# Low parts of the attention weights: an accumulating transfer in place of a subtraction on DVE

## The chip, the cores and the metric

The kernel runs on one core of one Trainium2 chip. The metric is the device time of one execution in microseconds (us), as a median over runs; less is better.

## The reference

Two blocks follow each other on 512 tokens of width 1024. The part that matters here is the first, a differential attention layer; the second is a feed-forward layer (ffn), a token mixer and another ffn, each added to x with a gate.

```python
def diff_attention_layer(x, norm_g, w_in, ..., w_out, layer_idx):
    h = rms_norm(x, norm_g)
    q, k, v, z = jnp.split(h @ w_in, 4, axis=-1)        # 1024 -> 4 x 2048
    q = rms_norm(q.reshape(b, s, 16, 2, 64), q_norm_g) * (64 ** -0.5)
    k = rms_norm(k.reshape(b, s, 16, 2, 64), k_norm_g)
    ...
    weights = probs[:, :, 0] - lam * probs[:, :, 1]     # two softmaxes a head
    ...
    o = o.reshape(b, s, BRANCH) * jax.nn.silu(z)
    return x + o @ w_out                                # 2048 -> 1024
```

Everything is float32.

## The kernel before

A product of two float32 matrices is made of three matmuls in the fp32r format: each operand is split into a high part, its rounding to fp32r, and a low part, what is left (`split`, line 105: ACT casts the high part, line 106; DVE subtracts it from the source, line 107). `mm3` (line 88) then adds high by high, high by low and low by high into one bank.

Weights come in tiles of 512 KB, 128 partitions by 1024 elements. `raw_w` (line 109) loads one on the queue of the engine SP into one of 3 buffers named raw; `split_w` (line 117) makes the tiles whi and wlo of it, of which there are 4 buffers each; `load_w` (line 114) does both. So a cast waits until PE has used the whi that lay in its buffer for the last time, and the next load of raw waits until the raw tile has been read.

Three shapes of products call `load_w`. `gemm_tok` (line 137) has tokens as output rows: with 4 weight tiles, it takes two of the four token tiles through all of the weights, then the other two, with 6 matmuls of 512 columns for each pair of a weight tile and a token tile. Where its argument `tail` is set, the last `tail` weight tiles are gone through one token tile after the other. `gemm_feat` (line 173) has features as output rows and uses each weight tile for 24 matmuls on end. `gemm_col` (line 187) is not used in attention.

The attention layer (line 633) starts with a hand-ordered first product (`start`, line 509, which splits its own weights at lines 560 and 567), and then makes four groups of four heads: `qk` for q and k (line 651), `vg` for v (line 718), `zg` for z (line 723), and `wo` for the output product (line 819). After a q or k product, ACT copies the result (line 671) and squares it, DVE sums, POOL raises the mean to the power -0.5 (line 305, tile rs) and scales the rows (line 678, tile qraw), both in POOL's one queue; PE transposes them later. v is copied by ACT (line 721), the output product is added to x by DVE (line 420). The scores, softmaxes and weighted sums of the group before (`attn`, line 735) are laid between the matmuls of these products.

The order of PE's work is set by the program: `tc.manual_schedule` holds for PE's engine alone, and `later` (line 67) with `spend` (line 71) puts the pieces of attention between the matmuls by a clock that counts matmuls (`self.now`) and the due times of `DL` (line 34). The other engines' order is made by the scheduler of the framework from the order in which the program issues and its own estimate of times. Each engine works through its queue in order. Transfers issued on POOL (`nc.gpsimd.dma_start`) stand in POOL's queue with its arithmetic; in attention these are the constants and the biases of the modulation (`bcast`, line 125).

Of the kernel before, what the change touches and what calls it, by code (L numbers as in the profile page):

```python
# [9 lines left out]
F32 = mybir.dt.float32  # L10
F32R = mybir.dt.float32r
AF = mybir.ActivationFunctionType
ALU = mybir.AluOpType
AX = mybir.AxisListType

P = 128
# [25 lines left out]
class Net:  # L42
# [4 lines left out]
    def __init__(self, ctx, tc, a):  # L47
        self.tc, self.nc, self.a = tc, tc.nc, a
        nc = self.nc
        pool = lambda name, bufs=1, **k: ctx.enter_context(tc.tile_pool(name=name, bufs=bufs, **k))  # L50
        self.const = pool("const")
        self.hp = pool("hp")
        self.wp = pool("wp", 4)
        self.wk = pool("wk", SLOTS)
        self.sp = pool("sp", 4)
        self.dram = pool("dram", 1, space=bass.MemoryType.DRAM)
        self.ps = pool("ps", 1, space=bass.MemoryType.PSUM)
        self.now, self.seq, self.tasks = 0.0, 0, []
        self.mod, self.ada_queue, self.ada_busy, self.scratch = {}, [], False, None

        self.ident = self.const.tile([P, P], F32, name="ident")
        self.mhalf = self.const.tile([P, 8], F32, name="mhalf")
        nc.vector.memset(self.mhalf, -0.5)
        self.x = [None] * NT
# [47 lines left out]
        return raw  # L112

    def load_w(self, src, kk, nn):
        return self.split_w(self.raw_w(src, kk, nn))

    def split_w(self, raw):
        _, kk, nn = raw.shape
# [748 lines left out]
    def ffn(self, s, win, wout, nxt):  # L867
        nc = self.nc
        sg, gT, gs = {}, {}, {}

        def gate(i):
            def done(bank, d0, d1):
                for o, d in ((d0[:, :256], bank), (d1, d1), (d0[:, 256:], d0[:, 256:])):
                    nc.scalar.activation(o, d, AF.Silu)
                sg[i] = d0, d1
            return done

        def up(i):
            def done(bank, *d):
                c = slice(0, 256), slice(256, 512)  # L880
                nc.vector.tensor_tensor(d[0][:, c[0]], bank, sg[i][0][:, c[0]], op=ALU.mult)
                nc.gpsimd.tensor_tensor(d[1], d[1], sg[i][1], op=ALU.mult)
                nc.gpsimd.tensor_tensor(d[0][:, c[1]], d[0][:, c[1]], sg[i][0][:, c[1]], op=ALU.mult)
                for n in range(2):
                    gT[2 * i + n] = d[n]
            return done

        if s == 2:
            self.ada(2, 2, 3.0)
        wts = [self.load_w(win[g * 512:(g + 1) * 512, c0:c0 + 256], 4, 256) for c0 in (0, FFN) for g in range(2)]  # L890
        sta = lambda n: lambda k: tuple(x[:, k % 4, n % 2 * P:n % 2 * P + P] for x in wts[n // 2 * 2 + k // 4])
        first = [self.tile("d0") for _ in range(2)]
        sg[0] = first

        def ev_up(n, bank):
            gT[n] = sg[0][n]
            nc.vector.tensor_tensor(gT[n], bank, gT[n], op=ALU.mult)

        self.gemm_quad([sta(n) for n in range(4)],
                       [lambda b, n=n: nc.scalar.activation(first[n], b, AF.Silu) for n in range(2)] +  # L900
                       [lambda b, n=n: ev_up(n, b) for n in range(2)])
        def split_g(k):
            if k not in gs:
                gs[k] = self.tile("gs", F32R), self.tile("gs", F32R)
                self.split(*gs[k], gT[k])

        def act(k, t):
            split_g(k)
            return tuple(g[:, t * P:(t + 1) * P] for g in gs[k])

        self.fast_feat([(win[:, c0 + i * 256:c0 + i * 256 + 256], fn(i))
                        for i in range(1, FFN // 256) for c0, fn in ((0, gate), (FFN, up))],
                       lambda: [split_g(k) for k in range(DL["gs"])])
        if s == 0:
            self.ada(1, 0, 2.5, True)
            self.ada(1, 1, 2.5, True)

        self.ada_wait((s, 2))
        self.norm_reset()
        for half in range(2):  # L920
            ev = self.gated_add(self.mod[s, 2], True, self.lazily(nxt) if half else None)
            self.gemm_tok(act, KF, wout[:, half * 512:half * 512 + 512], lambda t, b: ev(half, t, b), 4 if half else 0)
# [509 lines left out]
```

## Time and profile before

| | us |
|---|---|
| Median of 3 runs (1873.27 to 1878.37) | 1877.58 |
| The profiled execution | 1875.29 |
| Its span, first to last instruction | 1873.5 |
| PE busy | 1821.5 |
| DVE busy | 1405.7 |
| ACT busy | 929.3 |
| POOL busy | 393.4 |

Busy times overlap. PE is TensorE's matmuls, PEld its weight loads, DVE is VectorE, ACT ScalarE, POOL GpSimd; SP only issues transfers. A row of a group reads: line, engine, operation, out<-in by the program's names, the shapes, how often, busy time, mean ns of one, the idle time of the engine just before them, and after the arrow what ended it. In a timeline a row is the start, the length and the work, with the idle time before it in brackets. The granted clock is 1.00 for TensorE's upper level of 2.4 GHz and 0.50 for the lower of 1.2 GHz.

### The profile page before, as it was taken

The page shows a single profiled execution, that of the slowest core. Times are in us where ns is not written, and L with a number is a line of the kernel's source. Part 1 is how long each engine was busy: PE and PEld are TensorE (multiplying, and loading weights), DVE is VectorE, ACT ScalarE, POOL GpSimd, SP SyncE. Part 2 cuts the span into 40 slices and gives each one's busy share as a digit, 9 for nine tenths or more (in the row PEclk, how much of TensorE's full clock was granted, in tenths as well). Part 3 has the DMA queues.
Part 4 walks back from the last instruction along what each step waited for, and adds up shares of the span by engine and source line. Part 5 has one row for each costly group of instructions (what it writes and reads, how often), then busy time and mean ns, then how long its engine had stood idle before and what let it go on. Part 6 is the DMA issues. An engine that isn't in the chain of part 4 may idle for free.

```text
span 1873.5 us, 29082 instructions
## 1 busy us (share of the span) xinstructions
PE 1821.5 (97%) x10799; PEld 1604.6 (86%) x10799; DVE 1405.7 (75%) x2904; ACT 929.3 (50%) x1692; POOL 393.4 (21%) x376
## 2 busy tenths in 40 slices
PE   8999999999999999999999989999999999999997
PEld 5887878788888999998888778888888889999886
DVE  5568768776966899998365798787878789999633
ACT  5576575465653454553235745654433344554521
POOL 3213214042112122332030212212100112232000
PEclk9999999999999999999999999999999999999999
DMA  4534534625422233357324321222356333333331
GB/s 166 136 115 139 154 98 126 204 68 147 139 92 73 70 111 103 102 179 248 111 63 119 85 67 52 63 62 77 116 164 219 114 133 124 113 102 102 124 113 56
DMA packets 187618, 217.93 MB, mean 116 GB/s; under 512 B 9618, under 2 KB 129826, under 8 KB 187476
## 3 DMA queue, kind: packets, MB, share of 16 engines
q1 hardware_dynamic: 181892, 198.00, 34.8%
q0 software_dynamic: 5584, 18.08, 3.1%
q8 instruction: 85, 1.39, 0.3%
q14 instruction: 57, 0.47, 0.1%
HBM read 201.34 MB, written 2.11 MB: 109 GB/s over the span
## 4 chain that ended last, share of the span: by engine, by line
PE 81%; DVE 9%; issue 4%; ACT 2%; POOL 2%; DMA 2%; SPq 0%; POOLq 0%; DVEq 0%; ACTq 0%
PE acc L84 70%; PE sc L84 5%; DVE wlo L107 2%; PE av L84 2%; PE sc L95 2%; DVE cvy L1032 1%; PE tr L95 1%; PE tr L778 1%; POOL rs L305 1%; DMA raw<-in_l_w_in_dram 1%; PE tr L84 1%; DVE S L232 1%; DMA araw<-in_ada_w_dram 0%; ACT whi L106 0%; DVE hn L342 0%
## 5 line engine op out<-in xcount | busy, mean ns | idle before, releaser
L84 PE MATMUL acc<-hT,whi 128*128 128x256 f32 (+1 forms) x2704 | 642.2, 331 | 4.3 <-DVE d L266 2.8
L84 PEld LDWEIGHTS acc<-hT,whi 128*128 128x128 f32 x2704 | 447.4, 192 | 37.7 <-DVE d L266 3.2
L107 DVE TENSOR_TENSOR wlo<-raw,whi 128x1024 fp32r<-128x1024 f32 (+1 forms) x325 | 330.5, 1027 | 167.6 <-ACT whi L106 165.1
L84 PE MATMUL acc<-hT,wlo 128*128 128x256 f32 (+1 forms) x1352 | 440.8, 326 | 2.4 <-DVE wlo L107 2.3
L106 ACT CAST whi<-raw 128x1024 fp32r<-128x1024 f32 (+1 forms) x325 | 285.8, 880 | 314.1 <-PE acc L84 256.6
L84 PEld LDWEIGHTS acc<-hT,wlo 128*128 128x128 f32 x1352 | 258.4, 191 | 25.2 <-DVE wlo L107 3.4
L84 PE MATMUL acc<-whi,hT 128*128 128x512 f32 x768 | 268.1, 406 | 0.8 <-ACT hT L106 0.8
L305 POOL TENSOR_TENSOR rs<-ms,mhalf 128x8 f32<-128x8 f32 (+2 forms) x76 | 95.3, 1254 | 664.0 <-DVE ms L303 556.5
L84 PE MATMUL acc<-whi,gs 128*128 128x512 f32 x704 | 219.2, 390 | 1.8 <-DVE gs L107 1.8
L84 PE MATMUL acc<-T,whi 128*128 128x256 f32 x960 | 174.5, 283 | 0.0
L84 PEld LDWEIGHTS acc<-whi,hT 128*128 128x128 f32 x768 | 145.5, 190 | 31.4 <-DVE hT L107 1.9
L106 ACT CAST whi<-S 128x512 fp32r<-128x512 f32 x160 | 99.3, 621 | 117.5 <-DVE S L232 89.5
L84 PEld LDWEIGHTS acc<-whi,gs 128*128 128x128 f32 x704 | 132.0, 188 | 29.9 <-DVE gs L107 2.6
L84 PE MATMUL acc<-wlo,hT 128*128 128x512 f32 x384 | 151.6, 395 | 1.7 <-DVE wlo L567 1.7
L84 PEld LDWEIGHTS acc<-T,whi 128*128 128x128 f32 x960 | 149.7, 192 | 0.0
L107 DVE TENSOR_TENSOR wlo<-S,whi 128x512 fp32r<-128x512 f32 x160 | 140.4, 895 | 0.2 <-ACT whi L106 0.2
L84 PE MATMUL acc<-wlo,gs 128*128 128x512 f32 x352 | 137.0, 389 | 0.0
L84 PE MATMUL acc<-T,wlo 128*128 128x256 f32 x480 | 135.9, 283 | 0.0
L232 POOL TENSOR_TENSOR S<-raw,S 128x512 f32<-128x512 f32 x40 | 65.5, 1637 | 207.4 <-DVE S L232 188.1
L763 ACT ACTIVATE p<-p,mn 128x128 f32<-128x128 f32 (+3 forms) x128 | 71.1, 556 | 46.8 <-DVE mn L759 45.1
L84 PEld LDWEIGHTS acc<-T,wlo 128*128 128x128 f32 x480 | 92.1, 192 | 0.0
L467 DVE SCALAR_TENSOR_TENSOR aacc<-araw,silu_c,aacc 128x512 f32<-128x512 f32 x98 | 77.3, 788 | 13.8 <-DMA araw<-in_ada_w_dram 13.0
(294 smaller groups left out, 3086.1 us busy)
## 6 DMA issues: line engine op xcount, KB each, us to landing
raw<-in_ffn_w_in_dram SPq DMA_DIRECT2D x88, 512.0 KB, 3.6
raw<-in_l_w_in_dram SPq DMA_DIRECT2D x60, 512.0 KB, 4.0
araw<-in_ada_w_dram SPq DMA_DIRECT2D x112, 256.0 KB, 4.5
raw<-in_mix_w_in_dram SPq DMA_DIRECT2D x53, 512.0 KB, 3.9
raw<-in_ffn_w_out_dram SPq DMA_DIRECT2D x44, 512.0 KB, 3.7
raw<-in_l_w_out_dram SPq DMA_DIRECT2D x16, 512.0 KB, 3.7
ada<-in_ada_w_dram POOLq DMA_DIRECT2D x32, 256.0 KB, 4.0
ab<-in_ada_b_dram POOLq DMA_DIRECT2D x18, 256.0 KB, 3.9
```

Of the source, the lines that this page charges most:

```text
L84: self.nc.tensor.matmul(out, a, b, start=start, stop=stop, skip_group_check=onto)
L95: self.nc.tensor.transpose(out[:, j * P:(j + 1) * P], src(j), self.ident)
L106: return (self.nc.scalar.copy(hi, src), self.nc.vector.tensor_tensor(lo, src, hi.bitcast(F32), op=ALU.subtract))
L107: self.nc.vector.tensor_tensor(lo, src, hi.bitcast(F32), op=ALU.subtract))
L232: sub = lambda o, x, y, op=ALU.subtract, e=nc.vector: e.tensor_tensor(o, x, y, op=op)
L305: pin(nc.gpsimd.tensor_tensor(r[:, :n], ms[:, :n], self.mhalf[:, :n], op=ALU.pow))
L467: nc.vector.scalar_tensor_tensor(acc, raw, self.silu_c[:, k:k + 1], acc, op0=ALU.mult, op1=ALU.add)
L763: nc.scalar.activation(p_[m][:, :L], p_[m][:, :L], AF.Exp, bias=mn[:, m:m + 1], scale=-1.0, accum_out=st[:, m, b:b + 1])
L778: nc.tensor.transpose(tr[:, c * P:(c + 1) * P], p0[:, c * P:(c + 1) * P], self.ident)
L1032: nc.vector.scalar_tensor_tensor(y[:, j:], r[:, :S - j], cw[:, 3 - j, n:n + 1], y[:, j:], op0=ALU.mult, op1=ALU.add)
```

## The change

In attention, `load_w` no longer calls `split_w`. ACT casts the high part as before, and then writes the negated high part into the low part's tile. A transfer issued on POOL reads the weights from DRAM a second time and adds them to that tile. From the first ffn on (`ffn`, line 867) a flag sends `load_w` back to `split_w`; the weights of `start` and all that don't come through `load_w` stay as they were.

```diff
@@ __init__
         self.now, self.seq, self.tasks = 0.0, 0, []
+        self.by_dma = True
@@ load_w
     def load_w(self, src, kk, nn):
-        return self.split_w(self.raw_w(src, kk, nn))
+        raw = self.raw_w(src, kk, nn)
+        if not self.by_dma:
+            return self.split_w(raw)
+
+        hi = self.wp.tile([P, kk, nn], F32R, tag="whi", name="whi")
+        lo = self.wp.tile([P, kk, nn], F32R, tag="wlo", name="wlo")
+        self.nc.scalar.copy(hi, raw)
+        self.nc.scalar.mul(lo, hi.bitcast(F32), -1.0)
+        self.nc.gpsimd.dma_start(lo, src.rearrange("(k p) n -> p k n", p=P), accum_op=ALU.add)
+        return hi, lo
@@ ffn
+        self.by_dma = False
         if s == 2:
             self.ada(2, 2, 3.0)
```

## Rows read from the trace of the kernel before

**Rows 1.** The page: its span and PE's busy time.
```profile
span 1873.5 us, 29082 instructions
PE 1821.5 (97%) x10799; PEld 1604.6 (86%) x10799; DVE 1405.7 (75%) x2904; ACT 929.3 (50%) x1692; POOL 393.4 (21%) x376
```

**Rows 2.** A stretch: busy of PE, PEld, DVE, ACT, POOL; clock, DMA share, GB/s.
```profile
30.00:610.00 580.00, 565.66 (x2916) 475.72 (x2914) 410.83 (x869) 346.92 (x673) 146.41 (x114) 0.99 0.42 124
```

**Rows 3.** What PE waited for, 30 to 610 us: total, times, longest.
```profile
PE av L84 <- ACT wt L781: 5.3, 3, 2.1
PE tr L778 <- DVE qkl L695: 2.2, 1, 2.2
PE tr L778 <- DVE mn L759: 2.0, 1, 2.0
PE acc L84 <- DVE wlo L107: 1.4, 2, 1.1
PE sc L84 <- DVE qkl L695: 1.0, 1, 1.0
```

**Rows 4.** Groups of DVE and of ACT by shape, 30 to 610 us.
```profile
L107 DVE TENSOR_TENSOR wlo<-raw,whi 128x1024 fp32r<-128x1024 f32 x80 | 101.8, 1277 | 47.9 <-ACT whi L106 46.6 <-PE av L84 0.7
...
L106 ACT CAST whi<-raw 128x1024 fp32r<-128x1024 f32 x80 | 84.0, 1050 | 57.6 <-PE acc L84 52.9 <-DMA qkT<-qkT 1.7 <-DMA raw<-in_l_w_in_dram 1.5
```

**Rows 5.** Two stretches around 174 us, columns as in rows 2.
```profile
171.00:174.30 3.30, 1.28 (x11) 1.12 (x10) 3.27 (x9) 1.27 (x5) 2.19 (x2) 1.00 0.72 230
174.30:178.00 3.70, 3.70 (x11) 2.85 (x11) 2.67 (x10) 1.91 (x8) 0.00 (x0) 0.55 0.51 191
```

**Rows 6.** DMA queues and issues, 30 to 610 us; last number: us to landing.
```profile
q1 hardware_dynamic: 43016, 68.85, 40.5%
...
raw<-in_l_w_in_dram SPq DMA_DIRECT2D x57, 512.0 KB, 3.9
...
qkT<-qkl SPq DMA_DIRECT2D x32, 128.0 KB, 2.3
...
ab<-in_ada_b_dram POOLq DMA_DIRECT2D x6, 256.0 KB, 3.9
```

**Rows 7.** The chain that ended last, near 538 us.
```profile
538.21 14.98 PE acc L84 x66
```

**Rows 8.** Timeline of ACT, 36 to 60 us.
```profile
37.98 1.05 ACT L106 CAST whi<-raw 128x1024 fp32r<-128x1024 f32 x1 [1.00 <-PE acc L84]
...
51.58 0.59 ACT L671 COPY qraw<-acc 128x512 f32<-128x512 f32 x1 [5.68 <-PE acc L84]
```

**Rows 9.** Timeline of POOL, 30 to 60 us.
```profile
34.51 1.67 POOL L305 TENSOR_TENSOR rs<-ms,mhalf 128x8 f32<-128x8 f32 x1 [5.58 <-DVE ms L303]
...
39.98 2.62 POOL L305 TENSOR_TENSOR rs<-ms,mhalf 128x8 f32<-128x8 f32 x1
...
46.10 1.96 POOL L678 TENSOR_TENSOR qraw<-qraw,rs 128x512 f32<-128x512 f32 x1
```

**Rows 10.** Timeline of ACT, 56 to 90 us.
```profile
57.55 1.05 ACT L106 CAST whi<-raw 128x1024 fp32r<-128x1024 f32 x1
...
61.44 1.05 ACT L106 CAST whi<-raw 128x1024 fp32r<-128x1024 f32 x1
...
75.21 0.59 ACT L721 COPY v<-acc 128x512 f32<-128x512 f32 x1 [7.46 <-PE acc L84]
...
80.79 1.05 ACT L106 CAST whi<-raw 128x1024 fp32r<-128x1024 f32 x1
```

**Rows 11.** Timelines of ACT and of DVE, 564 to 582 us.
```profile
572.78 1.05 ACT L106 CAST whi<-raw 128x1024 fp32r<-128x1024 f32 x1
...
579.58 0.69 DVE L420 TENSOR_TENSOR x<-acc,x 128x512 f32<-128x512 f32 x1 [2.75 <-PE acc L84]
```

**Rows 12.** Instructions that read whi: ns of one, then first and last start.
```profile
L84 PEld LDWEIGHTS acc<-hT,whi x802: 186/192/193, 89.5 to 760.0; 128*128 128x128 f32 x161
```

**Rows 13.** Groups of POOL by shape, 30 to 610 us.
```profile
L125 POOL DMA_DIRECT2D ab<-in_ada_b_dram x6 | 3.7, 623 | 33.3 <-DVE co L767 21.6 <-PE sc L84 11.8
```

## The prediction, made before the changed kernel was run

> **What bounds the kernel now.** I read the page's busy times first: PE is busy for 1821.5 of 1873.5 us [rows 1]. Then a table by stage: in attention, taken here as 30 to 610 us of the span, PE is busy for 565.66 of 580 us, DVE for 410.83, ACT for 346.92, POOL for 146.41, and the DMA engines for 0.42 [rows 2]. So whatever DVE is relieved of, PE can give back 14 us at most here. Third, who PE waited for in that stretch [rows 3]: DVE in four lines (2.2, 2.0, 1.4 and 1.0 us, 6.6 together), ACT's copies of the transposed weights of attention in one (5.3 us). The low parts themselves (line 107) are the 1.4. The stage is bound by PE, and its order is fixed in the program, so that a late operand of PE is added to the time in full.
>
> **The change, part by part.** *Count.* load_w is called for 76 weight tiles before the first ffn switches the flag off: 28 for q and k without the first, 16 for v, 16 for z, 16 for the output product. The 80 casts and 80 subtractions in attention [rows 4] hold these and four of the ffn.
>
> *What goes.* 76 subtractions of 1.277 us [rows 4], 97 us of DVE. They lie beside PE's work. What PE gets back is between nothing and the 6.6 us of waits on DVE, plus a clock step: around 171 us PE stood for some 2 us behind DVE, and the next 3.7 us ran at a granted clock of 0.55, most of it at 1.2 GHz instead of 2.4 [rows 5], which costs 3.7 × 0.45 = 1.7 us. So 0 to 8.3 us; I take half, **-4**, since part of those DVE waits come from work that stays.
>
> *What ACT gets.* 76 negations of the same shape as the cast, 1.050 us each [rows 4]: 80 us on an engine with 233 us free in the stretch, beside PE's work. Each stands right behind its cast, so ACT's other work near a hand-over comes 1.05 us later. Next to be late are the copies that PE waits 5.3 us for [rows 3]. Bounds: none of it, or every one of the three waits longer by a cast and a negation (3 × 2.1 = 6.3); I take **+2.5**, as most copies stand far from a hand-over.
>
> *What POOL and the queues get.* 76 software-issued transfers of 512 KB on POOL's queue, which wait there for the negation. POOL's in-order work behind them is the normalization of q and k. No row shows an accumulating transfer. Nearest rows [rows 6]: 512 KB on SP's queue land in 3.9 us, 128 KB in 2.3, so 128 KB more cost 0.53 us, and 512 KB are 1.8 fixed plus 2.1 of data. A POOL transfer of 256 KB lands in 3.9 where SP's would take 2.8: 1.1 more. A plain 512 KB from POOL would then be 1.8 + 1.1 + 2.1 = 5.0 (estimate, low end; 3.9 if POOL cost nothing more). If the data part is paid for the weight, for the old low part and for the write back one after another, 1.8 + 1.1 + 3 × 2.1 = 9.2 (high end). I take two passes, **7.1 us**, because reading and writing overlap within any transfer and the second read does not obviously do so. The Trainium skill, "Collectives: The Full Stack", Why ReduceScatter is half of AllGather, says that an adding transfer costs no time for the add but needs two source reads, and so runs at half the rate; by it the landing would be the same 7.1, by a free second read 5.0, and no row here shows either.
>
> *Traffic.* SP's queue moves 68.85 MB in this stretch for 40.5% of the engines' time [rows 6]. 39.8 MB more, at once or twice that price, bring the DMA share from 0.42 to 0.65 or 0.89. The mean still fits; bursts are in the range's upper end.
>
> *The chain C.* Before, a low part was ready 2.3 us after its cast began (1.05, then 1.23 on DVE). Now: 1.05 + 1.05 + 0.1 + 7.1 = **9.3 us** (6.1 with the lowest landing, 11.4 with the highest).
>
> *What it meets.* Four buffers hold high and low parts. In a product by token tiles the cast waits for PE's last use of the buffer, and PE needs the next content 36 matmuls later; a matmul costs 14.98 / 66 = 0.227 us [rows 7], so 8.2 us, stretched by attention's own PE work in between. All 1824 matmuls of the 76 tiles take 414 of 580 us, so the mean stretch is 1.4 and the mean allowance 11.5 us, above 9.3. Where nothing lies between, it is below. Three places, each worked out from a cast and from the copy or addition that takes the result:
>
> - q to k, first hand-over. The cast starts at 37.98; the first result is copied at 51.58, 42 matmuls (9.5 us) after its first use at 42.0 [rows 8]. Allowance 4.0: stall 5.3. Besides, POOL works without a gap from 34.5 to 48.1 here; the first transfer could be issued at 40.1, in the middle of an instruction of 2.62 us [rows 9]. Bounds 0 to 8 us, by where it is queued; I take 2.5, the end of that instruction. Together **+7.8**.
> - k to v. Casts at 57.55 and 61.44, copy at 75.21, so first uses at 65.7 and 68.4 [rows 10]: allowances 8.1 and 7.0, stalls 1.2 and then 1.1 more. **+2.3**.
> - The last output product, second half: PE goes through all four new tiles for one token tile, so the third tile's cast at 572.78 is followed by its use at 579.58 - 12 × 0.227 = 576.9 [rows 11]. Allowance 4.1: **+5.2**.
> - Elsewhere: v to z gives 89.5 - 80.79 = 8.7 us [rows 10, 12], stall 0.6. Of the other hand-overs a few lie near 9 by a count of matmuls in the same manner. **+2** for all.
>
> *Clock.* A stand of 2 us was followed by the low clock level [rows 5]; two stalls of 5 us or more bring 2 × 1.7 = **+3.4**.
>
> *Sum:* -4 + 2.5 + 7.8 + 2.3 + 5.2 + 2 + 3.4 = +19.2. The profiled execution took 1875.3 (span 1873.5 and 1.8 around it), so 1894.5; it stands 2.3 below the median of 1877.6, so I forecast **1897** for the median.
>
> **The rivals.** *No loss (faster).* Mechanism: at the three hand-overs the second read is free and POOL is not in the way, so that a transfer lands like SP's in 3.9 us. C = 6.1 leaves stalls of 2.1 and 2.0 us, and DVE's whole 8.3 come back: -4.2, or 1873. It turns clearly faster only with a landing under about 3.5 us, and decides below that: C = 5.7, stalls of 1.7 and 1.6, about 1872. Against it stands the POOL transfer of half the size at 3.9 [rows 6].
>
> *No change.* One pass, landing 5.0, C = 7.2: stalls 3.2, 0.2 and 3.1, one clock step 1.7, less 6 from DVE: +2, so 1880.
>
> *POOL is late.* The transfers wait behind a normalization pair or are written slowly; 2.6 us more each (that long POOL instruction [rows 9]) make C = 11.9. Then the mean allowance of 11.5 is reached, and every product by token tiles stalls for 1 to 3 us, a good 20 more in ten of them, beside 2.6 more at each of the three places: 1897 + 30, about 1927. For it: POOL's in-order queue. Against it: POOL is a quarter busy [rows 2], and its transfers issue in 623 ns [rows 13]. The Trainium skill, "SBUF — State Buffer", Who interferes with whom, has POOL unable to write descriptors while DVE runs an instruction that takes both port pairs; by it the price would be of this kind, and no issue row here is stretched so.
>
> *Late everywhere.* Adding runs at a third of the rate or worse, landing 11.4 or more with the traffic: C = 13.6, 2 us over the mean allowance and 5 over the short ones, some 4 to 6 us in each of eleven products and ten at the three places: about 1955.
>
> That the change doesn't do what it says has no form I can find: the flag is a plain attribute, and every one of the 76 tiles passes through it.
>
> **How the numbers follow.** A measurement of this kernel tells a difference of about 0.3% (5.6 us) from none. Forecast (C of 7.5 to 10.5, 1884 to 1912): 0.48. POOL late: 0.18. Late everywhere: 0.13. No change: 0.14. No loss: 0.07, counted as faster. So faster 0.07, same 0.14, slower 0.79. The range 1877 to 1946 leaves out the faster case, a little of the no-change one, and most of the late one.
>
> **What would show it.** Right: DVE's busy time in attention falls by about 97 us, ACT's rises by 80; the accumulating transfers land in 6 to 8 us; PE's waits show POOL-queue transfers into the low parts, the longest near 40, 66 and 577 us, with half-clock rows behind them; the stages after attention keep their length. Wrong: landings of 4 us and PE waits no longer than before (no loss), or waits on low parts in every product and a DMA share near 0.9 (late everywhere), or POOL's normalizations on PE's path. If attention lengthens by 17 to 20 us but for other lines than these three places, the sum would be right by accident.

## The result, and the profile after

The changed kernel takes **1965.7 us** (median of 4 runs, 1965.4 to 1966.2) beside 1875.4 for the kernel before in the same comparison: ratio 1.0485, 95% interval 1.0471 to 1.0498. It is slower by 90 us, where some 20 were forecast; 1965.7 lies above the range, next to the rival "late everywhere" (1955).

The page, to be held against [rows 1]:

```profile
span 1964.4 us, 29241 instructions
...
PE 1849.9 (94%) x10799; PEld 1619.2 (82%) x10799; DVE 1314.6 (67%) x2828; ACT 1003.0 (51%) x1768; POOL 480.1 (24%) x452
```

The same 10799 matmuls cost PE 28 us more, and the span is 91 us longer; so most of the loss is time in which PE stands. Where, is read from busy time by stage, columns as in [rows 2]. Attention now reaches to about 698 us, so its stretch is 30 to 698, and the second line is all that follows.

```profile
30.00:698.00 668.00, 591.91 (x2885) 488.61 (x2884) 314.85 (x789) 419.56 (x748) 226.99 (x189) 0.94 0.72 166
698.00:1964.00 1266.00, 1236.94 (x7843) 1117.07 (x7841) 986.24 (x2012) 569.21 (x988) 249.13 (x254) 0.99 0.36 111
```

What is to be seen: nearly all of the loss lies in attention, 668 us for the 580 of [rows 2]; what follows took 1263.5 us before. DVE's busy time fell by 96 us and ACT's rose by 73. PE now stands for 76 us of the stretch (668 - 591.91) where it stood for 14, 62 more; and about as many matmuls (2885 for 2916) keep it busy for 26 us more, at a granted clock that fell from 0.99 to 0.94. The DMA share rose from 0.42 to 0.72.

What the new load_w does, in the groups by shape of attention (against [rows 4]):

```profile
L123 ACT ACTIVATE wlo<-whi 128x1024 fp32r<-128x1024 f32 x76 | 80.4, 1057 | 1.2
L122 ACT CAST whi<-raw 128x1024 fp32r<-128x1024 f32 x76 | 79.4, 1047 | 41.6 <-PE acc L85 29.9 <-DMA raw<-in_l_w_in_dram 8.4 <-DMA raw<-in_l_w_out_dram 2.8
L124 POOL DMA_DIRECT2D wlo<-in_l_w_in_dram x60 | 74.2, 1266 | 204.6 <-ACT wlo L123 154.9 <-PE acc L85 29.1 <-ACT wt L791 7.5
```

The negations take the 80 us that were counted. The cast now waits 11.2 us for raw weights as well (8.4 and 2.8), where it waited 1.5 for the first of them.

What PE waited for in attention, to be held against [rows 3]:

```profile
PE acc L85 <- DMA wlo<-in_l_w_in_dram: 26.3, 11, 8.2
PE av L85 <- ACT wt L791: 11.1, 3, 7.2
PE acc L85 <- DMA wlo<-in_l_w_out_dram: 10.7, 5, 6.2
PE sc L85 <- DVE qkl L705: 6.4, 1, 6.4
PE tr L788 <- DVE qkl L705: 5.0, 1, 5.0
PE acc L85 <- DVE mn L769: 4.7, 1, 4.7
PE sc L85 <- DVE mn L769: 3.6, 1, 3.6
```

The low parts stop PE for 37.0 us in 16 stands. As much again, 39 us, are waits on DVE and ACT, on the same softmax and transposition work as in [rows 3], and the longest of them are now several us long. That second half is what a look at the low parts alone would miss.

The DMA queues and issues of attention (against [rows 6]; q0 is POOL's queue, q1 SP's):

```profile
q0 software_dynamic: 25488, 42.21, 37.3%
q1 hardware_dynamic: 42354, 68.19, 34.5%
...
wlo<-in_l_w_in_dram POOLq DMA_DIRECT2D x60, 512.0 KB, 8.0
raw<-in_l_w_in_dram SPq DMA_DIRECT2D x57, 512.0 KB, 5.2
araw<-in_ada_w_dram SPq DMA_DIRECT2D x48, 256.0 KB, 4.5
```

Here araw are the loads of the modulation: while attention runs, its weights come in pieces of 256 KB on SP's queue, and DVE adds each piece into a sum (aacc) that the first ffn needs later. 42 MB on POOL's queue take more of the engines than 68 MB on SP's: 37.3% of 668 us is 249 us of all 16 engines, or 5.9 us of all 16 per MB, against 3.4 on SP's queue, 1.75 times as much. Medians hide what this does to others. The ranges (least, median, most) are: low parts 6.0, 8.0 and 13.9 us; raw weights 3.4, 5.1 and 13.7, where the most was 6.2 before; modulation loads (araw) 2.8, 4.5 and 12.8, where the most was 5.3.

Stands of PE on low parts, in timelines of PE and, for the first, of ACT and POOL; the number in brackets is how long PE stood before the instruction:

```profile
40.14 1.06 ACT L123 ACTIVATE wlo<-whi 128x1024 fp32r<-128x1024 f32 x1
...
43.77 3.78 POOL L124 DMA_DIRECT2D wlo<-in_l_w_in_dram  x3
...
51.56 0.80 PE L85 MATMUL acc<-wlo,hT 128*128 128x512 f32 x1 [8.22 <-DMA wlo<-in_l_w_in_dram]
...
80.82 0.80 PE L85 MATMUL acc<-wlo,hT 128*128 128x512 f32 x1 [3.18 <-DMA wlo<-in_l_w_in_dram]
...
216.96 0.80 PE L85 MATMUL acc<-wlo,hT 128*128 128x512 f32 x1 [3.31 <-DMA wlo<-in_l_w_in_dram]
...
668.01 0.79 PE L85 MATMUL acc<-wlo,oghi 128*128 128x512 f32 x1 [6.20 <-DMA wlo<-in_l_w_out_dram]
```

The stands at 51.56, 80.82 and 668.01 are the three places of the prediction. The matmul that follows a long stand takes 0.80 us where such a one takes 0.39 in full clock.

One of the other stands, followed back. SP issues a modulation load, DVE waits for it, DVE's next work comes late, PE waits for that (timeline of all engines, 165 to 184 us):

```profile
165.22 4.66 SPq L112 DMA_DIRECT2D raw<-in_l_w_in_dram  x2
...
169.94 0.57 SPq L472 DMA_DIRECT2D araw<-in_ada_w_dram  x1
...
179.44 0.75 DVE L477 SCALAR_TENSOR_TENSOR aacc<-araw,silu_c,aacc 128x512 f32<-128x512 f32 x1 [5.30 <-DMA araw<-in_ada_w_dram]
...
180.96 1.52 DVE L705 SCALAR_TENSOR_TENSOR qkl<-tr,cols,qkT 64x512 fp32r<-64x512 f32 x2
...
182.63 0.66 PE L85 MATMUL sc<-qkT 128*128 128x384 f32 x1 [6.37 <-DVE qkl L705]
```

From its issue to its use the load takes 9.5 us, where such a load landed in 4.2 before (median). DVE does its work in the order of its queue, so it stands 5.3 us at a modulation sum, which the scores don't need, and the query and key parts queued behind it hold PE for 6.4. Such waits of DVE for modulation loads are 59.4 us in 17 in attention; before they were 9.9 in 8.

Last, stretches of PE's two long stands above and of what came after each, columns as in [rows 2]:

```profile
43.00:52.00 9.00, 0.78 (x3) 0.44 (x2) 1.04 (x2) 4.98 (x7) 8.44 (x7) 0.66 0.99 234
52.00:56.00 4.00, 4.00 (x11) 3.03 (x10) 0.00 (x0) 0.00 (x0) 0.00 (x0) 0.50 1.10 236
176.00:183.00 7.00, 0.64 (x3) 0.41 (x2) 3.43 (x7) 1.52 (x2) 2.23 (x2) 0.71 1.10 277
183.00:187.00 4.00, 4.00 (x14) 3.25 (x14) 2.77 (x8) 2.41 (x5) 0.24 (x1) 0.65 0.97 257
```

In both stands the DMA engines are full (0.99 and 1.10 by this count), and PE runs the first 4 us after them at a granted clock of 0.50 and 0.65, all or most of it at 1.2 GHz.

So after the first reading there are three theories, named in the expectations by a letter. **W**: PE waits for late low parts. **T**: the second transfers fill the DMA engines, and what lands late for it, loads that have nothing to do with the low parts, makes DVE or ACT late. **A**: ACT's 80 us of negations.

### The profile page after: what moved, and what is told of

It is laid out like the page before. It is cut to its first block, busy times and chain, and to the rows that moved or that the text cites. A ratio compares the mean times of both kernels' runs of the same rounds, so it can differ in the third digit from the quotient of the medians.

```text
span 1964.4 us, 29241 instructions
## 1 busy us (share of the span) xinstructions
PE 1849.9 (94%) x10799; PEld 1619.2 (82%) x10799; DVE 1314.6 (67%) x2828; ACT 1003.0 (51%) x1768; POOL 480.1 (24%) x452
## 5 line engine op out<-in xcount | busy, mean ns | idle before, releaser
L107 ACT CAST whi<-raw 128x512 fp32r<-128x512 f32 (+1 forms) x249 | 205.9, 829 | 256.6 <-PE acc L85 198.6
L108 DVE TENSOR_TENSOR wlo<-raw,whi 128x512 fp32r<-128x512 f32 (+1 forms) x249 | 234.3, 951 | 119.4 <-ACT whi L107 118.0
L85 PE MATMUL acc<-whi,hT 128*128 128x512 f32 x768 | 276.1, 417 | 3.3 <-DVE o L805 2.1
L85 PE MATMUL acc<-wlo,hT 128*128 128x512 f32 x384 | 158.2, 412 | 25.3 <-DMA wlo<-in_l_w_in_dram 22.2
L85 PEld LDWEIGHTS acc<-whi,hT 128*128 128x128 f32 x768 | 151.2, 197 | 35.5 <-DVE o L805 2.5
L124 POOL DMA_DIRECT2D wlo<-in_l_w_in_dram x60 | 74.2, 1266 | 204.6 <-ACT wlo L123 154.9
L85 PEld LDWEIGHTS acc<-wlo,hT 128*128 128x128 f32 x384 | 75.9, 198 | 42.6 <-DMA wlo<-in_l_w_in_dram 27.1
```

The costliest lines, as they stand in the source:

```text
L85: self.nc.tensor.matmul(out, a, b, start=start, stop=stop, skip_group_check=onto)
L107: return (self.nc.scalar.copy(hi, src), self.nc.vector.tensor_tensor(lo, src, hi.bitcast(F32), op=ALU.subtract))
L108: self.nc.vector.tensor_tensor(lo, src, hi.bitcast(F32), op=ALU.subtract))
L124: self.nc.gpsimd.dma_start(lo, src.rearrange("(k p) n -> p k n", p=P), accum_op=ALU.add)
```

## The experiments

All times are medians; each ratio is against the kernel before in the same comparison, with its 95% interval. 14 runs are told; the kernel before measured 1874.5 to 1875.8 in all of them.

### The transfer taken out, or only made cheaper

**The addition done by DVE.** ACT's negation stays; the second transfer goes.

```diff
-        self.nc.gpsimd.dma_start(lo, src.rearrange("(k p) n -> p k n", p=P), accum_op=ALU.add)
+        self.nc.vector.tensor_tensor(lo, raw, lo.bitcast(F32), op=ALU.add)
```

> The negation by ACT stays, and DVE adds the weights to it; there is no second transfer, nothing else is changed. The low part is then ready 1.05 + 1.05 + 1.23 us after the cast begins, 1.1 us later than in the kernel before, and below every allowance. Theory W (PE waits for low parts that land late) and theory T (the second transfers fill the DMA engines and make the other transfers late) both expect the time of the kernel before, 1875 to 1882. Theory A (ACT's 80 us more are what delays attention's own work) expects a good part of the 39 us of other waits, 1890 or more.

Measured 1886.1, 1.0052 (1.0037 to 1.0067): 10 us, between what W and T expected (1875 to 1882) and what A expected (1890 or more). The loads land as before (medians 3.8 and 4.0 us, at most 7.2). ACT's negations, with DVE's addition left where the subtraction was, are a tenth of the loss. The copies of the transposed weights, where [rows 3] had PE's wait for ACT, show 2.4 us of it (7.7 us in 4 waits, 5.3 in 3 before); the rest is in no one line.

**The same transfer without its addition** (left out: the addition; the low part is then the weight itself).

```diff
-        self.nc.gpsimd.dma_start(lo, src.rearrange("(k p) n -> p k n", p=P), accum_op=ALU.add)
+        self.nc.gpsimd.dma_start(lo, src.rearrange("(k p) n -> p k n", p=P))
```

> The transfer on POOL stays, but copies the weights over the low part and adds nothing (the addition is left out). Same chain, same queue, same issue. If the second read and the addition are what makes it long, the landing falls from 8.0 us to 5 to 5.5, the chain to about 7.5, and theory W expects 10 us of stalls on low parts in place of 37, with their clock steps; theory T expects POOL's queue to take 22% of the DMA engines' time in attention in place of 37% and the other waits to fall from 39 to 10 or 15 us. Together 1895 to 1910. If the price is the software queue's and not the addition's, landing and time stay (1950 or more).

Measured 1919.7, 1.0236 (1.0217 to 1.0255). A plain copy from POOL's queue lands in 5.8 us, 2.2 less than the adding one, and stops PE for 20.6 us where the adding one stops it for 37.0. The engines do their work in the order of the changed kernel. So the adding costs half of the loss (46 us), and a kernel with plain second copies loses the other half (44), more than the 20 to 35 that were expected: the second copies are too many even without the adding.

**The transfer for the 16 z tiles only.**

```diff
-        if not self.by_dma:
+        if not self.by_dma or kk != 4:
```

> Only the 16 weight tiles of z, which PE uses one after the other and whose allowances are 11 us and more but for the first, get their low parts by transfer; the other 60 by DVE. Theory W: one stall of about 2 us at v to z, the rest hidden, 16 subtractions less on DVE: 1874 to 1880. Theory T: the transfers still collide with the others where they run, 16/76 of about 50 us: 1884 to 1890.

Measured 1891.4, 1.0083 (1.0066 to 1.01). A fifth of the transfers cost a sixth of the loss. PE waits only 1.9 us for low parts here, but a modulation load still lands as late as 12.7 us, and DVE waits 20.5 us for them. The time is a little above what T expected (1884 to 1890) and 11 us above W's range. So W can't be all of it.

### Traffic that nobody waits for

The kernel before, with its subtractions on DVE, and 76 accumulating transfers of the high parts into four buffers in DRAM that nothing reads (the first four of them only copy).

```diff
-        return self.split_w(self.raw_w(src, kk, nn))
+        hi, lo = self.split_w(self.raw_w(src, kk, nn))
+        if self.by_dma:
+            sink = self.sinks[self.turn_ % 4]
+            self.turn_ += 1
+            self.nc.gpsimd.dma_start(sink.rearrange("p (k n) -> p k n", k=kk), hi.bitcast(F32), **(dict(accum_op=ALU.add) if self.turn_ > 4 else {}))
+        return hi, lo
```

> The kernel before, plus one accumulating transfer of 512 KB for each of the 76 tiles, issued on POOL as soon as the cast is done: it adds the high part to one of four DRAM tiles that nobody reads (the first four only copy). Low parts come from DVE as before, so PE never waits for these transfers. Theory W expects the time of the kernel before, 1875 to 1882. Theory T expects the other waits and their share of half-clock time: 39 us and some 13, so 1915 to 1930, with the modulation's loads landing late and PE's waits put to DVE and ACT.

Measured 1939.5, 1.0336 (1.0318 to 1.0353): 64 us from transfers that nobody waits for, more than T expected (1915 to 1930). DVE, ACT and SP do the same work in the same order as in the kernel before; besides the traffic only POOL's 65 us of issuing are new. What PE and then DVE waited for in attention (total, times, longest):

```profile
PE av L86 <- ACT wt L788: 15.5, 4, 6.1
PE tr L785 <- DVE qkl L702: 10.1, 1, 10.1
PE acc L86 <- DVE o L802: 9.3, 1, 9.3
```

```profile
DVE aacc L474 <- DMA araw<-in_ada_w_dram: 43.4, 14, 9.4
DVE aacc L472 <- DMA araw<-in_ada_w_dram: 27.0, 5, 10.2
```

No transfer is in PE's list. DVE waits 70.4 us for modulation loads, and PE for what stands behind them on DVE. That points at the way by which T costs time; it doesn't show it yet, since the raw weights land late too (median 6.7 us).

### Is it the modulation loads? Three edits

**Issued one step ahead**, meant to give a load longer to land. The edit, here of the changed kernel; the same was made to the kernel before and to the one with unread transfers:

```diff
-        def one(k, half, acc):
+        def fetch(k, half):
...
+            return raw
+
+        def one(k, half, acc, raw=None):
+            c0 = s * 3 * D + kind * D + half * 512
+            raw = raw or fetch(k, half)
+            nxt = None
+            if s == 0 and (k < KD - 1 or half == 0):
+                nxt = fetch((k + 1) % KD, half + (k == KD - 1))
...
-                self.later(step, lambda: one(k + 1, half, acc))
+                self.later(step, lambda: one(k + 1, half, acc, nxt))
```

The changed kernel:

> The changed kernel, with the loads of the modulation's weights in attention issued one step (6 or 3 us of PE's time) before the step that uses them. Traffic and chain of the low parts stay. Theory T, in the form that late modulation loads hold DVE's queue and with it the scores: DVE's wait for them falls from 59 us to under 20, the 39 us of other PE waits to under 15, and the time to 1915 to 1930. If these loads are not the way, 1955 or more.

The kernel before:

> The kernel before with the same earlier loads. DVE waited 9.9 us for them there, and one PE stand of 2.7 us near 355 us with its clock step was put to them: 1869 to 1875, a gain of up to 6 us, or none if the stand only moves to another wait.

The kernel before with transfers that nobody waits for:

> The kernel before plus the 76 transfers that nobody waits for, with the earlier loads. If the late modulation loads were what cost the 64 us there, 1885 to 1900; if the weights' own loads and the transfers across halves of q and k were late as well, 1910 to 1930.

Measured: 1957.6 (ratio 1.0443, 1.0426 to 1.0461), 1865.1 (0.9949, 0.9936 to 0.9962) and 1920.4 (1.0247, 1.023 to 1.0265). Each gains 8 to 19 us, the kernel before as much as the changed one. (The stand near 355 us that the second expectation names is 2.1 us long in the trace of the kernel before, at 358.4, and a copy of ACT ended it.) DVE's waits for the loads hardly fall (55.4 us of 59.4 in the changed kernel, 67.6 of 70.4 with unread transfers), because the edit didn't do what it was meant to. From a load's issue to the moment at which DVE was free for its sum the median is 6.9 us in the changed kernel, where it was 7.0 (5.8 for 5.1 in the kernel before, 6.7 for 6.7 with unread transfers): the scheduler put the sums earlier in DVE's order too, by up to 20 instructions. So this edit could not decide the question. What it shows is the price of another order with the same waits: the unread transfers cost 55 us there (1920.4 against 1865.1), 64 without the edit. In the changed kernel PE's other waits fell from 39 to 27 us, but those on low parts rose from 37.0 to 50.4: a stand for one reason gives the low parts time to land, and where it goes another comes out. The edit did give a kernel that beats both (below).

**Issued from ACT's queue**, so that no load stands behind weight loads in SP's.

```diff
-            (nc.gpsimd if scratch else nc.sync).dma_start(raw, ...
+            (nc.gpsimd if scratch else nc.scalar if s == 0 else nc.sync).dma_start(raw, ...
```

> The changed kernel with the modulation loads of attention issued from ScalarE's queue in place of SyncE's, which carries the weight loads. If the loads are late because they stand behind weight loads in SyncE's queue: their landing returns to about 4 to 5 us at the maximum 7, and the time falls to 1930 to 1950. If they are late because all 16 DMA engines are full (Theory T as stated): landing keeps its maximum of 10 us and more, time 1950 to 1970; each issue on ScalarE may add some us. Theory W: 1960 to 1970.

Measured 1959.9, 1.0454 (1.0439 to 1.047): the 6 us are a fifteenth of the loss. The latest landing falls from 12.8 to 9.2 us, but the median rises from 4.5 to 5.1 and DVE still waits 61.2 us, in 24 waits. The place in SP's queue makes the worst landings worse; it isn't the only reason why they are late, since 9.2 is still far above the 5.3 of the kernel before. The 6 us themselves say little: on ACT's queue the loads were also issued later, 4.0 us (median) before DVE was free for them in place of 7.0, and PE's waits on low parts rose from 37.0 to 45.6 us.

**The sums on a resident tile.** DVE's modulation sums in attention keep their number and shape, but read a tile that is already there; the loads are still made, and no sum waits for them (left out, in this and in all kernels named "resident": the true modulation values of the first ffn).

```diff
+        hT = self.hT[0] if s == 0 else None
...
+            if s == 0:
+                raw = hT[:, k, :].bitcast(F32)
```

The kernel before, as the control:

> Control: the kernel before with the modulation sums of attention on a resident tile (left out: the true modulation values of the first feed-forward). VectorE waited 9.9 us for these loads in the kernel before. Every theory: 1862 to 1876, like the kernel before with its modulation loads one step ahead (1865.1). If it falls further, the gains of the two runs beside it are to be read against this one, not against the kernel before.

The kernel before with transfers that nobody waits for:

> The kernel before plus 76 accumulating transfers that nobody waits for (1939.5 us), with the modulation sums of attention on a resident tile (left out: the true modulation values of the first feed-forward). Theory T by way of the modulation sums: most of the 64 us go, 1880 to 1900. Theory T by way of late weight loads: 1910 to 1940, with PE's waits now on ScalarE's casts. Theory W has no late low parts here and gave no account of the 64 us; it expects nothing of this edit.

The changed kernel:

> The changed kernel, in which VectorE's modulation sums during attention read a resident tile in place of the loaded modulation weights; the loads are still made, so the traffic is the same (left out: the true modulation values of the first feed-forward). The changed kernel took 1965.7 us; its PE waited about 37 us for low parts and about 39 us for other things, mostly VectorE's and ScalarE's softmax work. Theory W (late low parts alone): 1955 to 1966, PE's other waits stay near 39. Theory T by way of the modulation sums (a late modulation load holds VectorE, and the softmax work is queued behind it): PE's other waits fall below 15 us and the time to 1915 to 1940. Theory T by way of the weight loads alone (late raw weights hold ScalarE's cast): 1950 to 1966. Theory A (ScalarE's extra work): 1955 to 1966.

Measured: control 1861.6 (0.9929, 0.9912 to 0.9945); unread transfers 1877.7 (1.0016, 1.0006 to 1.0026); changed kernel 1932.6 (1.031, 1.0295 to 1.0325); the first two lie just under what was expected. These are the runs that tell most. Against their own controls the same unread transfers cost 64 us with the true sums and 16 without, although the traffic is the same and the loads land as late (modulation loads 7.2 us in the median and at most 13.7, beside 6.7 and 14.1 with the true sums). **Late landings cost little, 16 us, as long as DVE's modulation sums don't wait for them in the middle of attention.**

One thing stays mixed in. A sum that waits for no load is also put elsewhere by the scheduler: in all resident kernels the 48 sums stand earlier in DVE's order, by 21 of its other instructions in the median and up to 73. Within a pair (control and unread transfers) DVE's order is the same, so 64 and 16 are clean. How much of the 48 us between them is the missing wait and how much the new place isn't separated; where the sums moved by up to 20 instructions and kept their waits (one step ahead), 55 of the 64 us stayed, which speaks for the waits. And one wait of several us of DVE for a modulation load is left in two of these kernels, ahead of a softmax instruction: 6.7 us in the changed kernel, 7.8 in its version below with the low part unread.

What PE waited for with the unread transfers, and then in the changed kernel, both with resident sums:

```profile
PE sc L86 <- DVE x L427: 4.2, 1, 4.2
PE av L86 <- ACT wt L791: 4.1, 3, 2.4
```

```profile
PE acc L85 <- DMA wlo<-in_l_w_in_dram: 31.9, 14, 8.6
PE acc L85 <- DMA wlo<-in_l_w_out_dram: 11.1, 5, 7.1
PE av L85 <- ACT wt L794: 8.0, 2, 5.1
```

In the first the waits on DVE of 10.1 and 9.3 us are gone. In the second the waits on low parts are left (43.0 us, 37.0 before this edit), and the others fall from 39 to 14.

### What waiting for the low parts is worth

The changed kernel keeps negation and transfer, but PE multiplies by the high part where it multiplied by the low one (left out: the low parts of attention's weights in the product), so that nobody waits for the transfer. Once with the true modulation sums, once with resident ones.

```diff
-        return hi, lo
+        return hi, hi
```

> The changed kernel with its negation and its accumulating transfer as they are, but TensorE multiplies by the high part where it multiplied by the low part (left out: the low parts of attention's weights in the product), so nobody waits for the transfer. Theory T with A (late modulation loads and ScalarE's work make the time whatever is done with the low parts): the 64 us of transfers that nobody waits for and about 10 us of ScalarE, 1935 to 1955. Theory W (waiting for the low parts is most of the 90 us): 1885 to 1915.

> The same, with the modulation sums of attention on a resident tile as well (left out: the low parts in the product, and the true modulation values of the first feed-forward). Theory W for the rest: the control's 1861.6, 16 us of traffic and about 10 us of ScalarE, 1880 to 1900, so that waiting for low parts is worth 35 to 50 us where the sums are not in the way. Theory A (ScalarE's negations, once traffic delays what they wait for, are the rest): 1915 to 1935.

Measured 1922.7 (1.0245, 1.0223 to 1.0266) and 1881.2 (1.003, 1.0016 to 1.0044). The first falls between what T with A expected and what W expected: each is about half of the truth. The longest waits of PE in the second:

```profile
PE av L85 <- ACT wt L794: 7.4, 4, 3.6
PE sc L85 <- DVE x L430: 3.3, 1, 3.3
```

With these, the 90 us divide (medians, us):

| | true sums | resident sums |
|---|---|---|
| low parts by DVE (the kernel before) | 1875.4 | 1861.6 |
| unread transfers, subtraction kept on DVE | 1939.5 | 1877.7 |
| negation and transfer, low part unread | 1922.7 | 1881.2 |
| the changed kernel | 1965.7 | 1932.6 |

- **PE's waits for late low parts, with the slow clock after them:** 1965.7 - 1922.7 = 43 (51 by the other column). In both pairs the engines' order of work is all but the same.
- **Modulation sums that hold DVE:** 1922.7 - 1881.2 = 41.5, of which the kernel before has 13.8 already: 28 (19 by the rows of the changed kernel). Their new place in DVE's order is in it.
- **The rest of the traffic and ACT's negations:** 1881.2 - 1861.6 = 20, of which 16 are there without a negation. The 3.5 left hold ACT's negations, the subtractions that DVE no longer has, and the difference between writing to DRAM and to the low parts; no run separates these.

43 + 28 + 20 is 91, with the 90.3 measured; the brackets, 51 + 19 + 20, are the same division taken in the other order. Not settled: unread transfers into DRAM with the subtraction on DVE cost 17 us more than the kernel with negation and unread low parts (1939.5 against 1922.7). DVE has 96 us less to do in the second, but the first also writes to another place; nothing separates the two.

### The negation before the cast

```diff
-        self.nc.scalar.copy(hi, raw)
-        self.nc.scalar.mul(lo, hi.bitcast(F32), -1.0)
+        self.nc.scalar.mul(lo, raw, -1.0)
         self.nc.gpsimd.dma_start(lo, src.rearrange("(k p) n -> p k n", p=P), accum_op=ALU.add)
+        self.nc.scalar.copy(hi, raw)
```

> The changed kernel, with the negation made from the weights themselves and ahead of the cast, so that the transfer can start 1.05 us sooner. Theory W: each of the about 16 stalls on low parts is up to 1 us shorter, 37 us falls to 25, with fewer clock steps: 1945 to 1955. If full DMA engines set when a low part lands, nothing is gained: 1960 to 1968.

Measured 1951.7, 1.042 (1.0401 to 1.0438). Starting each transfer about 1 us sooner gains 14 us, a sixth of the loss, as W expected in number, but not by W's way. PE's waits on low parts fall only from 37.0 to 34.5 (26.6 and 7.9), where 25 were expected, and the three longest are 9.4, 5.4 and 5.3 us; DVE's waits for modulation loads stay (56.0). The rest of the gain lies in PE's other waits (39 to 30 us) and its busy time (4 us less over the whole span). ACT's work has another order here; why the other waits fell isn't shown.

### The version that beats both

It is the kernel before with its modulation loads issued one step ahead: 1865.1, 0.5% faster than the kernel before (0.9949, 0.9936 to 0.9962, 6 runs). What PE waited for in attention:

```profile
PE tr L786 <- DVE qkl L703: 2.3, 1, 2.3
PE av L84 <- ACT wt L789: 1.6, 1, 1.6
```

The copies of the transposed weights are down from 5.3 us to 1.6, and the wait of 2.0 on the softmax's row minimum is gone [rows 3]. DVE's waits for the loads are no shorter in sum (12.3 us, 9.9 before), and the loads have hardly more time (5.8 us for 5.1), so the gain goes with the new order of DVE's work; which move makes it stays open. The control without any such wait stands at 1861.6; little more is to be had in this way.

## Why the prediction was wrong

The sign was right, the size was not: 20 us forecast, 90 measured. By the prediction's steps:

- **Count, relief, what ACT gets.** Right as counts: 76 negations at 1.06 us (80.4 us on ACT), DVE's busy time down by 96. The prices can't be told apart: -4 and +2.5 were forecast, 3.5 us are left for both where nobody waits for a transfer or for DVE's sums, and ACT's negations cost 10 where DVE keeps an addition. No gain from the relief shows in PE's waits on DVE, which grew.
- **Landing.** 7.1 forecast, 8.0 measured. The step from one pass to two was right: plain 5.8, adding 8.0, a difference of 2.2 for the 2.1 taken. Both stand 0.8 to 0.9 above the estimate, which was made from rows of engines 0.42 busy. The Trainium skill, "Collectives: The Full Stack", Why ReduceScatter is half of AllGather, gives the adding step of a ReduceScatter two source reads and half the rate of a copy. Here the direction agrees, and the rate is less than halved: the adding transfer takes 1.75 times the engine time per MB of SP's queue, and by the shares and MB of POOL's queue (37.3% of 668 us for 42.21 MB, against 26.1% of 620 us for 42.08 MB of plain copies) 1.54 times a plain copy of the same queue. One step of the estimate doesn't hold: SP's queue was said to land 256 KB in 2.8 us, so that POOL's 3.9 cost 1.1 more, but the view of [rows 6] has 48 loads of that size on SP's queue, and they land in 4.2:

```profile
araw<-in_ada_w_dram SPq DMA_DIRECT2D x48, 256.0 KB, 4.2
```

- **The chain C.** This step failed. 9.3 us were forecast from the start of the cast to the landing; worked out tile by tile from the trace it is 11.5 in the median (8.5 to 16.7), which is the mean allowance. Its mean, 11.65, is 2.35 too long: 1.3 in the landing (8.4 in the mean), 0.55 because ACT does other work between cast and negation, 0.5 because POOL is at other work. With plain copies the chain is 9.1 in the median, about the forecast, and there the low parts stop PE for 20.6 us, where the forecast's stalls sum to 17.3.
- **First hand-over, k to v, last output product.** +7.8, +2.3 and +5.2 were forecast; PE stood 8.2, 3.2 and 6.2 us there. The allowances were right: 4.3, 8.3 and 4.2 us, for 4.0, 8.1 and 4.1. The first and the last were right for the reason given, POOL's busy stretch included (negation done at 41.2, transfer issued at 43.77). At k to v the size is in part luck: one stand in place of two, with 1.4 us of ACT's other work between cast and negation.
- **Elsewhere, +2.** It failed with C. Of the 37.0 us on low parts 19.4 lie at other hand-overs, 13 of them, of 0.8 to 3.3 us. The mean allowance of 11.5 us was set against one landing of 7.1; with landings up to 13.9, a hand-over with the mean allowance is late whenever its transfer falls into a burst. A mean on both sides hid that.
- **Traffic: "The mean still fits; bursts are in the range's upper end."** This is the step that cost most. The share was foreseen (0.65 to 0.89, measured 0.72), and its price was put at nothing. It made some 28 us by way of the modulation sums on DVE and 16 more that no sum carries. The prediction never asked which other loads land on the same engines, and what waits for them: the modulation loads appear in none of its rows. In the kernel before they landed within 5.3 us, and DVE waited 9.9 us for them, which was the sign to look for.
- **Clock, +3.4.** Mis-sized: PE's busy time in attention grew by 26 us. The price for one step was about right (in 52 to 56 us, 4 us at 0.50 lose 2.0; 1.7 was taken); the number of stands wasn't. Two stands of 5 us or more were counted; there are eleven of 3 us or more, seven of them not on low parts.
- **POOL is late.** Its number is the nearest to the chain (11.9, measured 11.5), and so is what it drew from it: a good 20 us more in stalls of 1 to 3 us, where 19.4 were found. Its cause is a small part: 9 of the 76 transfers were issued 1.6 to 2.7 us after their negation had ended, behind normalizations and other work of POOL. An issue takes 1.2 us where a plain copy of the same size takes 0.74 and 256 KB took 0.62 [rows 13], so it is the adding that makes it longer.
- **Late everywhere.** Nearest in time, and half right in mechanism. Low parts are late at 16 hand-overs, though adding doesn't run at a third of the rate; what the rival lacked, late work of DVE behind late loads, is not in its text, so that its 1955 is near by luck.

Put into one sum: low parts with their clock 43 instead of 21 (7.8 + 2.3 + 5.2 + 2 + 3.4), traffic 44 instead of 0, ACT and relief together 3.5 instead of -1.5.

## What to carry to other kernels

Before more traffic is put on the DMA engines, list every load that shares them and who waits for each, in the order of its engine's queue: a load that lands 9 us late costs little where nothing in order stands behind its consumer, and several us of the bounding engine where something does. Set an allowance against the latest landing under the new load, not against the median before the change. And a mean DMA share of 0.7 says little: look at the share in the stretch of each hand-over, which was 0.99 and 1.10 in the two stands shown. Last, check that an edit meant to move or free a piece of work left the order of the rest alone; here the scheduler moved the sums with their loads.

## What was not expected of the hardware

- A transfer that adds in place takes 5.9 us of all 16 DMA engines per MB, counted over the queue, against 3.4 on SP's queue for plain loads; its landing is 8.0 us for 512 KB against 5.8 for a plain copy from the same queue in the same kernel, and its issue on POOL takes 1.2 us against 0.74.
- 76 such transfers of 512 KB raise the latest landing of 256 KB loads on another queue from 5.3 to 12.8 us, and moving those loads to a third queue brings it down only to 9.2, with a higher median.
- Late landings by themselves are cheap: with raw weights and modulation loads landing at up to 14 us the kernel lost 16 us over its control (0.9%), with no modulation sum on DVE waiting for them.
